# TensorE's order in block 1 written out by hand, with a new head and softmax attention by pairs of heads

## The chip, the core and the metric

One core of a Trainium2 chip runs the whole program. The metric is the device time of one execution in microseconds (us). Five engines work side by side, each through its own instructions in order: TensorE (PE in the profile, its weight loads as PEld), VectorE (DVE), ScalarE (ACT), GpSimd (POOL) and SyncE (SP), which issues most DMAs. This chip can tell differences of about 0.2% of this kernel's time from no change.

## The reference, cut to what matters

Two transformer blocks run on 256 tokens of width 2048, batch 1. Block 1 puts 16 meta tokens in front (272 rows), and everything is float32:

```python
xn = _rms(h, n1)
z_rwkv, z_fox, z_gate = jnp.split(xn @ w_in, (RWKV_COLS, RWKV_COLS + FOX_COLS), axis=-1)
y_a = _rwkv7(z_rwkv + (z_prev - z_rwkv) * mu, ...)   # 16 heads of 64: S = S*w + (S a) b^T + v k^T
y_b = _fox(z_fox, ...)                               # 16 heads of 64: causal softmax with a decay bias
merged = g_a * (y_a @ w_a) + g_b * (y_b @ w_b)       # gates of z_gate
h = h + merged @ w_o
h = h + (silu(gate) * up) @ w_dn                     # gate, up of _rms(h) @ w_gu
```

Block 2 (projections, stick-breaking and chunked softmax attention, an output projection) follows and is not touched.

## The kernel before, in words

Every large product is made of three single-pass matmuls of split operands (`mm3`): `wload` brings 512 KB of weights by a DMA of SP's queue into a `raw` tile (three of them), ACT casts it to `hi`, and DVE subtracts to get `lo` (`split`, lines 219 to 221). `hi` and `lo` have three buffers each. `gemm_a` makes one 128-column tile of a projection, transposed (48 matmuls of 272 columns or fewer, from two chunks of 24); `gemm_b` makes 512 output columns (96 matmuls of 512 columns from eight chunks). Products that are not split are plain float32 matmuls, which the trace shows as two instructions each.

Block 1 works in this order (lines 290 to 813). The head loads the normalised input's raw form and the first weights (`first`: 112, then 96 columns), and builds `xh`/`xl`, the split input. Each of the three later `first` tiles follows only when the one before has its weights. The row norm `rs` is taken out of the matmul and multiplied in afterwards. Then come four groups `q` of four heads: `rwkv(q)` makes six projection tiles, the decays, 4 x 4 x 2 blocks of inner products (`gt`), a triangular inverse of 31 dependent steps on DVE (lines 570 to 582, between two rounds of DMA through DRAM), and then a recurrence over one short and four long stretches (lines 625 to 678). Each stretch is a chain TensorE, DVE, TensorE, ACT and DVE, TensorE, DVE. A group norm (lines 687 to 702), four transposes and a DMA to `ydr` end it. `fox(q)` makes six more tiles and goes through its four heads one after the other: scores, softmax, five transposes, and five small products per head (lines 750 to 787). `gate(n)` are eight `gemm_b` groups. After that, `w_b` and `w_a` multiply the two branches, which come back from `ydr`.

What sets the order: Tile's scheduler. It plays a timeline over all engines and gives each engine, at each moment, the instruction of highest priority that is ready by its estimates; priority is the order of tracing, and weight loads are moved ahead by 300. So TensorE's order, too, comes from the estimates, and small products are strewn between the matmuls of a tile wherever the planner had them ready.

PSUM has four banks for projections (`g`), two for the recurrence (`q`) and two for softmax attention (`f`).

Of the kernel before, what the change touches and what calls it, by code (L numbers as in the profile page):

```python
# [15 lines left out]
D = 2048  # L16
# [7 lines left out]
AHEAD = 300  # L24
BANKS = {"g": 4, "q": 2, "f": 2}
# [82 lines left out]
def prep(i):  # L108
# [51 lines left out]
    l0 = np.concatenate([w[:, 3072:3168], w[:, 6592:6608]], 1)  # L160
    a["w_l0"] = A(l0.reshape(2, 8, 128, 112).transpose(0, 2, 1, 3))
    a["w_l1"] = A(w[:, 3168:3264].reshape(2, 8, 128, 96).transpose(0, 2, 1, 3))
    sel = [w[:, 3264:3520]]
# [33 lines left out]
def body(tc, a, out):  # L197
# [5 lines left out]
    with ExitStack() as top:  # L203
# [21 lines left out]
        def wload(src, n, m, ahead=AHEAD, dst=None, parts=1):  # L225
# [7 lines left out]
            with tc.high_priority(offset=ahead):  # L233
                for i in range(parts):
                    ns, fs = slice(i * n // parts, (i + 1) * n // parts), slice(i * f // parts, (i + 1) * f // parts)
                    latest[0] = nc.sync.dma_start(r3(raw)[:, ns], src[:, ns])  # L236
                    split(raw[:, fs], hi[:, fs], lo[:, fs])
            return r3(hi), r3(lo)

        def mm(o, l, r, start=True, stop=True, **k):  # L240
            P.matmul(o, l, r, start=start, stop=stop, **k)  # L241

# [5 lines left out]
        def gemm_a(chunks, kpc, x, m, n, ready=False):  # L248
            ps = bank("g")
            nk = len(chunks) * kpc  # L250
            for ci, src in enumerate(chunks):
                w = src if ready else wload(src, kpc, m)
# [37 lines left out]
        with ExitStack() as ph:  # L290
            x3 = ph.enter_context(tc.tile_pool(name="x3", bufs=1))
            rp = ph.enter_context(tc.tile_pool(name="rp", bufs=1))
            NTMP, RT0 = 7, META - 2
# [4 lines left out]
            def tmpf(shape):  # L298
                return T(rp, shape, "c", bufs=5)
# [4 lines left out]
            def tmpp(shape):  # L304
                return T(rp, shape, "p", bufs=4)

# [3 lines left out]
            first, xs_ = [], []  # L310
            for j, src in enumerate((a["w_l0"][0], a["w_l0"][1], a["w_l1"][0], a["w_l1"][1])):
                xr = x4()[:, :4 * L].rearrange("p (k t) -> p k t", t=L)
                step = 2 if j == 0 else 4
                for i0 in range(0, 4, step):
                    nc.sync.dma_start(xr[:, i0:i0 + step], a["xT"][:, 4 * j + i0:4 * j + i0 + step])
                    if i0 == 0:
                        first.append(wload(src, 8, 112 if j < 2 else 96, ahead=0, parts=4 // step))
                    for i in range(i0, i0 + step):
# [3 lines left out]
                S.activation(xr, xr, AF.Square)  # L322
                G.tensor_tensor(out=xr[:, 0:2], in0=xr[:, 0:2], in1=xr[:, 2:4], op=ALU.add)
                G.tensor_tensor(out=xr[:, 0], in0=xr[:, 0], in1=xr[:, 1], op=ALU.add)
                xs_.append(xr)
            G.dma_start(ident, a["eye"])
            G.dma_start(ones, a["one"])
            G.dma_start(cst, a["cst"])
            ps = bank()
            for j in range(4):  # L330
                mm(ps[:, :L], ones, xs_[j][:, 0], j == 0, j == 3)
            rs = T(rp, [128, L], "rs")
            S.activation(rs, ps[:, :L], AF.Sqrt, bias=e6, scale=1.0 / D)
            V.reciprocal(rs, rs)
            ps = bank()
            rsn = T(cp, [128, 4], "rsn")
            for t in range(2):
                P.transpose(ps[:, 128 * t:128 * t + 128], rs[:, META + 128 * t:META + 128 * t + 128], ident)
            V.tensor_copy(rsn[:, 0:2], ps[:, 0:256].rearrange("p (t c) -> p t c", c=128)[:, :, 0])
            V.tensor_scalar(out=rsn[:, 2:4], in0=rsn[:, 0:2], scalar1=0.5, scalar2=None, op0=ALU.mult)  # L340
# [10 lines left out]
            xk = lambda kt: (xh[:, kt], xl[:, kt])  # L351
# [22 lines left out]

            lz = T(rp, [128, L], "lz", bufs=2)
            ps = gemm_a(first[:2], 8, xk, 112, L, True)
            shift(ps, 112, 0, lz[:112])
# [18 lines left out]
            ps = bank()  # L396
            for t in range(2):
                P.transpose(ps[:, 16 * t:16 * t + 16], fz[fr, 1, META + 128 * t:META + 128 * t + 128], ident[fr, fr])
            V.tensor_copy(cq, ps[:, :32].rearrange("p (a b) -> p a b", b=16))

            lz = T(rp, [128, L], "lz", bufs=2)
            ps = gemm_a(first[2:], 8, xk, 96, L, True)
            shift(ps, 96, 1, lz[:96])
# [3 lines left out]
            for j in range(2):  # L407
                lz = T(rp, [128, L], "lz", bufs=2)
                shift(next_a(RT0), 128, 2 + j, lz[:, META:], RT0)
# [6 lines left out]
            def to_units(src, dst, tag):  # L416

                ps = bank(tag)
                for j in range(2):
                    for t in range(2):  # L420
                        P.transpose(ps[:, 256 * j + 128 * t:256 * j + 128 * t + 128], src[:, t, 128 * j:128 * j + 128], ident)
                ys = T(rp, [128, 512], "ys" + tag)
                S.copy(ys, ps)
                G.dma_start(dst, ys)

# [5 lines left out]
            def rwkv(q):  # L431
# [7 lines left out]
                for j in range(2):  # L439
                    shift(next_a(), 128, 8 + 6 * q + j, vz[:, j, 48:])  # L440
# [765 lines left out]
```

## Time and profile before

| what | us |
|---|---|
| median of three timed runs | 2049.92 (2048.58 to 2051.02) |
| the profiled execution | 2047.9 |
| its span, first to last instruction | 2046.1 |
| PE busy in the span | 2003.9 (98%) |
| DVE busy | 1223.2 (60%) |
| ACT busy | 954.9 (47%) |
| POOL busy | 156.8 (8%) |

Busy time of PE counts matmuls to their modelled end, so a PE that is busy may still run small products that fill it badly, or run at a lower clock. How well a stretch is used is read from the distance between starts of matmuls. In this trace block 1, with `w_b`, takes the first 731 us; `w_a` starts at 753.

### The profile page before, as it was taken

What the parts mean: (1) busy time and instruction counts of PE and PEld (TensorE: products, weight loads), DVE (VectorE), ACT (ScalarE), POOL (GpSimd) and SP (SyncE); (2) the same over time, 40 slices, a digit from 0 to 9 for tenths busy, and PEclk for the clock granted to TensorE, in tenths of its full rate; (3) what the DMA queues carried; (4) which work ended last, traced back from release to release, by engine and by line L of the source; (5) the groups of instructions that cost most, each with busy time, mean ns of one, the idle gap of its engine ahead of it and who ended that gap; (6) DMA issues with size and microseconds to landing.
All of it is one profiled execution on the core that took longest, in us unless ns stands there. A gap on an engine that the chain in (4) does not pass through costs nothing.

```text
span 2046.1 us, 29715 instructions
## 1 busy us (share of the span) xinstructions
PE 2003.9 (98%) x11478; PEld 1719.1 (84%) x11478; DVE 1223.2 (60%) x2161; ACT 954.9 (47%) x1285; POOL 156.8 (8%) x230
## 2 busy tenths in 40 slices
PE   8999999999999959999999999999999999999998
PEld 7999889889878748888888888888888888998886
DVE  6686777678557547555555544555555565665555
ACT  6545454545444324454444433444444555444443
POOL 3122221231110100000000000000000000000000
PEclk9999999999989979999999999999999999999999
DMA  5544455355446647555555555555555565444554
GB/s 190 184 153 140 147 173 159 126 159 159 139 143 212 227 160 250 188 187 188 192 189 186 193 191 193 194 192 189 186 193 186 180 204 187 146 142 155 183 193 145
DMA packets 118847, 363.28 MB, mean 178 GB/s; under 512 B 28800, under 2 KB 29088, under 8 KB 118704
## 3 DMA queue, kind: packets, MB, share of 16 engines
q1 hardware_dynamic: 113712, 344.98, 51.3%
q0 software_dynamic: 4992, 16.40, 2.6%
q8 instruction: 90, 1.47, 0.3%
q14 instruction: 53, 0.43, 0.1%
HBM read 351.72 MB, written 9.60 MB: 177 GB/s over the span
## 4 chain that ended last, share of the span: by engine, by line
PE 95%; DMA 1%; ACT 1%; issue 1%; DVE 1%; SPq 0%; DVEq 0%; POOL 0%; ACTq 0%; POOLq 0%
PE g L241 85%; PE f L241 4%; PE q L241 4%; DMA raw<-in_w_a 1%; PE q L833 1%; PE f L833 1%; DMA x<-in_xT 0%; ACT hi L220 0%; DVE lo L221 0%; DMA raw<-in_w_b 0%; PE q L559 0%; DVE X L321 0%; SPq L236 0%; PE f L1086 0%; PE q L1086 0%
## 5 line engine op out<-in xcount | busy, mean ns | idle before, releaser
L221 DVE TENSOR_TENSOR lo<-raw,hi 128x1024 fp32r<-128x1024 f32 (+2 forms) x633 | 771.6, 1220 | 611.4 <-ACT hi L220 608.6
L241 PE MATMUL g<-hi,X 128*128 128x512 f32 (+1 forms) x3344 | 1048.5, 392 | 12.6 <-ACT hi L220 12.4
L220 ACT CAST hi<-raw 128x1024 fp32r<-128x1024 f32 (+2 forms) x633 | 661.4, 1045 | 851.7 <-PE g L241 724.7
L241 PEld LDWEIGHTS g<-hi,X 128*128 128x128 f32 x3344 | 626.7, 189 | 143.5 <-issue 16.0
L241 PE MATMUL g<-lo,X 128*128 128x512 f32 (+1 forms) x1672 | 656.3, 393 | 0.9 <-DVE lo L221 0.9
L241 PE MATMUL g<-X,hi 128*128 128x272 f32 (+4 forms) x2176 | 429.7, 293 | 9.1 <-ACT hi L220 5.9
L241 PEld LDWEIGHTS g<-lo,X 128*128 128x128 f32 x1672 | 315.3, 189 | 66.0 <-DVE lo L221 2.5
L241 PEld LDWEIGHTS g<-X,hi 128*128 128x128 f32 (+2 forms) x2176 | 346.7, 191 | 15.8 <-ACT hi L220 5.9
L241 PE MATMUL g<-X,lo 128*128 128x272 f32 (+3 forms) x1088 | 320.6, 295 | 0.0
L241 PEld LDWEIGHTS g<-X,lo 128*128 128x128 f32 (+1 forms) x1088 | 207.6, 191 | 2.7 <-issue 0.7
L241 PE MATMUL g<-hi,Y 128*128 128x512 f32 x544 | 170.9, 390 | 0.0
L241 PEld LDWEIGHTS g<-hi,Y 128*128 128x128 f32 x544 | 102.2, 188 | 20.7
L241 PE MATMUL g<-lo,Y 128*128 128x512 f32 x272 | 106.6, 392 | 0.0
L945 POOL DMA_DIRECT2D cst<-in_cst x1 | 0.5, 543 | 832.8 <-PE g L241 832.8
L241 PEld LDWEIGHTS g<-lo,Y 128*128 128x128 f32 x272 | 51.1, 188 | 10.3
L761 POOL TENSOR_SCALAR p<-ckb,cq,qs 128x144 f32<-128x144 f32 (+1 forms) x32 | 42.9, 1347 | 46.4 <-issue 31.1
L582 DVE TENSOR_TENSOR c<-c 108x42 f32<-108x42 f32 (+31 forms) x236 | 40.5, 206 | 0.3
L579 DVE TENSOR_TENSOR c<-hq,c 108x42 f32<-108x42 f32 (+31 forms) x236 | 39.5, 202 | 1.1 <-DMA hq<-hd 0.9
L367 POOL TENSOR_TENSOR d<-z 128x272 f32<-128x272 f32 (+3 forms) x28 | 23.3, 834 | 136.7 <-DVE z L366 101.7
L768 ACT ACTIVATE p<-p,fst,qs 128x144 f32<-128x144 f32 (+1 forms) x32 | 17.7, 555 | 23.4 <-DVE fst L767 23.0
L241 PEld LDWEIGHTS q<-x,x 64*128 64x128 f32 (+1 forms) x160 | 17.7, 189 | 4.9 <-issue 2.9
L645 POOL TENSOR_TENSOR sp<-sbd,pp 64x128 f32<-64x128 f32 x24 | 14.7, 612 | 88.2 <-DVE sbd L671 57.7
(448 smaller groups left out, 1411.9 us busy)
## 6 DMA issues: line engine op xcount, KB each, us to landing
raw<-in_w_gu SPq DMA_DIRECT2D x176, 512.0 KB
raw<-in_w_A SPq DMA_DIRECT2D x100, 512.0 KB
raw<-in_w_dn SPq DMA_DIRECT2D x88, 512.0 KB
raw<-in_w_g SPq DMA_DIRECT2D x64, 512.0 KB
raw<-in_w_o SPq DMA_DIRECT2D x32, 512.0 KB
raw<-in_w_qk SPq DMA_DIRECT2D x32, 512.0 KB
raw<-in_w_out SPq DMA_DIRECT2D x32, 512.0 KB
raw<-in_w_b SPq DMA_DIRECT2D x16, 512.0 KB
```

Source lines behind the costliest of these rows:

```text
L220: S.copy(hi, src)
L221: V.tensor_tensor(out=lo, in0=src, in1=hi.bitcast(F32), op=ALU.subtract)
L241: P.matmul(o, l, r, start=start, stop=stop, **k)
L367: G.tensor_tensor(out=d[:m, t1:], in0=z[:m, t1:L], in1=z[:m, 1 + t1:], op=ALU.subtract)
L579: V.tensor_tensor(out=t_, in0=hs[:108, j, j + 1:].unsqueeze(1).to_broadcast([108, k_, w]), in1=xs[:, :, j:j + 1].to_broadcast([108, k_, w] ...
L582: V.tensor_tensor(out=xs[:, :, j + 1:], in0=xs[:, :, j + 1:], in1=t_, op=ALU.add)
L645: G.tensor_tensor(out=sp[64 * e:64 * e + 64], in0=blk_(old, e), in1=dec(e), op=ALU.mult)
L761: G.tensor_scalar(out=m_, in0=ckb[:, h, :n], scalar1=cq[:, t, hg:hg + 1], scalar2=qs[:, 0, t, h:h + 1], op0=ALU.subtract, op1=ALU.mult)
L768: S.activation(sm[:, rng[t]], sm[:, rng[t]], AF.Exp, bias=st[:, 1, sidx:sidx + 1], scale=qs[:, 1, t, h:h + 1], accum_out=st[:, 2, sidx:sid ...
L833: P.transpose(ps[:, o:o + 128], src[:, t, 128 * (k + j):128 * (k + j) + 128], ident)
L945: G.dma_start(cst2, a["cst2"])
```

## The change

- **TensorE's order.** Within block 1, `tc.manual_schedule` keeps TensorE's instructions in the order of tracing. The other engines are scheduled as before. The parts of `rwkv` and `fox` that follow the projections become generators. `now` adds up an estimated TensorE time; a generator yields the time after which its next products may be placed, and after every `mm3` of a `gemm` the program resumes those that are due.
- **Order of the large work.** For each q: six tiles of `rwkv`, spawn its task, six tiles of `fox`, spawn its task, then the gates: none, 4, 5, and 6, 7, 0, 1, 2, 3. `turn` keeps two recurrences from overlapping. What is left over after the last gate is placed there.
- **Head.** The first three tiles are made together (weights `w_f`, 336 columns, in eight loads), row by row as input and weights arrive, with three matmuls of zeros ahead of them. The norm becomes a task, and the constants go by SP's queue.
- **Softmax attention** works on pairs of heads: scores of both heads alternate, the probabilities are normalised on DVE before they are transposed, the meta tokens of both heads share one product (`vpad`, `vd`), and the output comes out transposed, so `to_units` is not needed for it.
- **Buffers.** `xx`, `gnw` and `ysf` have their own tiles; tag `c` has four buffers, not five.

```diff
+GATES = ((), (4,), (5,), (6, 7, 0, 1, 2, 3))
+        now, tasks = [0.0], []
+        def pump():
+            while True:
+                due = [k_ for k_ in tasks if k_[0] <= now[0]]
+                if not due:
+                    return
+                k_ = min(due, key=lambda k_: k_[0])
+                try:
+                    k_[0] = now[0] + next(k_[1])
+                except StopIteration:
+                    tasks.remove(k_)
+        def spawn(task):
+            tasks.append([now[0], task])
+            pump()
         def mm(o, l, r, start=True, stop=True, **k):
             P.matmul(o, l, r, start=start, stop=stop, **k)
+            now[0] += (12 + int(np.prod(r.shape[1:])) * (1 if r.dtype == F32R else 4) / 2.4) / 1e3
                     mm3(ps[:m, :n], [t[:, j] for t in w], x(kt), kt == 0, kt == nk - 1)
+                    pump()
+            ph.enter_context(tc.manual_schedule(engines={mybir.EngineType.PE}))
+            wz = tmpf([128, 512])
+            V.memset(wz, 0.0)
+            ps = bank()
+            for _ in range(3):
+                mm(ps, wz[:, :128], wz)
+            FIRST = ((0, 112, 0), (112, 96, 0), (208, 128, RT0))
+            pf = [bank("g") for _ in FIRST]
...
+                        for p_, (c0, m, t0) in zip(pf, FIRST):
+                            mm3(p_[:m, :L - t0], [t_[:, i - i0, c0:c0 + m] for t_ in w], (xh[:, kt, t0:], xl[:, kt, t0:]), kt == 0, kt == 15)
...
+            def rwkv(q, kz, rz, vz):
                 wl = wload(a["w_lora"][q], 4, 256)
+                yield 2.0
...
+                yield 9.0
...
+                yield 14.0
+                while turn[0] != q:
+                    yield 1.0
...
+                yield 46.0
...
+                        yield 1.8
...
+                        yield 1.6
...
+                    yield 2.4
+                turn[0] = q + 1
...
+                yield 16.0
                 to_units(yf, ydr[0][q], "q")
...
+                    yield 3.0
+                    sc = [bank("f") for _ in range(2)]
                     for t in range(2):
+                        for e in range(2):
+                            er = slice(64 * e, 64 * e + 64)
+                            mm(sc[e][:, rng[t]], qn[er, j, 128 * t:128 * t + 128], kn[er, j, :144 + 128 * t])
...
+                    yield 11.0
...
+                    yield 2.2
+                    yb = bank("f")
+                    mm(yb[:, :256], vd[:, 128 * j:128 * j + 128], pm, True, False, skip_group_check=True)
+                    for e in range(2):
+                        mm(yb[64 * e:64 * e + 64, :256], vn[:, 0, 128 * j + 64 * e:128 * j + 64 * e + 64], pts[e][:, 0:256], False, False, skip_group_check=True)
+                    for e in range(2):
+                        mm(yb[64 * e:64 * e + 64, 128:256], vn[:, 1, 128 * j + 64 * e:128 * j + 64 * e + 64], pts[e][:, 256:384], False, True, skip_group_check=True)
...
+            for q, gates in enumerate(GATES):
+                spawn(rwkv(q, *rwkv_in(q)))
+                spawn(fox(q, *fox_in()))
                 for n in gates:
                     gate(n)
+            while tasks:
+                now[0] += 0.5
+                pump()
```

## Rows read from the trace of the kernel before

**Rows 1.** The page: busy us, share of the span, instructions, by engine.

```profile
PE 2003.9 (98%) x11478; PEld 1719.1 (84%) x11478; DVE 1223.2 (60%) x2161; ACT 954.9 (47%) x1285; POOL 156.8 (8%) x230
```

**Rows 2.** TensorE's waits: for what, us in total, times, longest.

```profile
PE q L241 <- DVE g__2826 L651: 1.4, 1, 1.4
```

**Rows 3.** Windows: stretch, us, then busy us of PE, PEld, DVE, ACT, POOL, granted clock, DMA.

```profile
0.00:20.00 20.00, 10.87 (x35) 8.14 (x36) 11.41 (x25) 13.01 (x24) 8.08 (x17) 1.00 0.72 248
...
100.00:150.00 50.00, 50.00 (x396) 47.48 (x394) 43.20 (x151) 22.86 (x36) 12.86 (x12) 1.00 0.50 155
...
350.00:400.00 50.00, 48.63 (x370) 44.55 (x369) 33.35 (x61) 26.55 (x41) 7.50 (x11) 0.93 0.39 134
...
550.00:600.00 50.00, 50.00 (x258) 37.84 (x256) 23.67 (x55) 18.17 (x35) 8.51 (x13) 0.90 0.38 120
...
700.00:750.00 50.00, 31.85 (x181) 24.90 (x179) 24.52 (x41) 13.29 (x20) 2.99 (x6) 0.83 0.43 145
```

**Rows 4.** Timeline of TensorE, head: start, us, what, count, idle before and its releaser.

```profile
5.87 0.80 PE L241 MATMUL g<-X,hi 128*112 128x272 f32 x2 [5.87 <-ACT hi L220]
...
21.62 0.88 PE L241 MATMUL g<-X,hi 128*96 128x272 f32 x3
22.30 0.43 PE L241 MATMUL g<-X,lo 128*96 128x272 f32 x1
...
24.30 0.41 PE L241 MATMUL g<-X,hi 128*96 128x272 f32 x2
24.55 0.29 PE L241 MATMUL g<-X,lo 128*96 128x272 f32 x1
...
42.41 0.42 PE L241 MATMUL g<-X,hi 128*128 128x272 f32 x2
```

**Rows 5.** Timeline of ACT in the head.

```profile
17.61 0.82 ACT L220 CAST hi<-raw 128x768 fp32r<-128x768 f32 x1
18.34 1.76 ACT L320 ACTIVATE X<-x,vec 128x272 fp32r<-128x272 f32 x4
20.00 1.09 ACT L322 ACTIVATE x<-x 128x1088 f32<-128x1088 f32 x1
```

**Rows 6.** One window of the head; the last number is the DMA rate in GB/s.

```profile
12.00:14.00 2.00, 1.16 (x3) 0.63 (x3) 1.74 (x2) 1.88 (x4) 1.92 (x2) 1.00 1.03 412
```

**Rows 7.** Timeline of TensorE: one head's small products, then the next head's scores.

```profile
147.33 0.43 PE L241 MATMUL f<-vm,p 16*128 16x64 f32 x2
...
149.00 0.97 PE L241 MATMUL f<-f 64*128 64x144 f32 x4
149.90 0.51 PE L241 MATMUL g<-X,hi 128*128 128x258 f32 x2
```

**Rows 8.** Timeline of TensorE: products whose neighbours use other halves of the array.

```profile
107.55 1.16 PE L241 MATMUL q<-x,x 64*128 64x128 f32 x16
108.64 0.40 PE L241 MATMUL g<-X,hi 128*128 128x272 f32 x1
...
718.50 0.45 PE L241 MATMUL q<-uv,kb 128*64 128x64 f32 x8
718.78 0.40 PE L241 MATMUL q<-uv,gt 128*64 128x64 f32 x6
```

**Rows 9.** Timeline of TensorE, end of block 1.

```profile
730.35 0.81 PE L241 MATMUL q<-uv,gt 128*64 128x64 f32 x8 [0.36 <-ACT uv L656]
...
753.26 1.19 PE L241 MATMUL g<-hi,X 128*128 128x512 f32 x2 [12.44 <-ACT hi L220]
```

**Rows 10.** Timeline of ACT where the gates give way to `w_b`.

```profile
684.12 1.05 ACT L220 CAST hi<-raw 128x1024 fp32r<-128x1024 f32 x1 [4.04 <-DMA raw<-in_w_b]
```

**Rows 11.** The page's costliest groups: count, busy us, mean ns, idle before.

```profile
L221 DVE TENSOR_TENSOR lo<-raw,hi 128x1024 fp32r<-128x1024 f32 (+2 forms) x633 | 771.6, 1220 | 611.4 <-ACT hi L220 608.6
L582 DVE TENSOR_TENSOR c<-c 108x42 f32<-108x42 f32 (+31 forms) x236 | 40.5, 206 | 0.3
L579 DVE TENSOR_TENSOR c<-hq,c 108x42 f32<-108x42 f32 (+31 forms) x236 | 39.5, 202 | 1.1 <-DMA hq<-hd 0.9
```

More of the change, by code (lines that the diff above doesn't have):

```diff
@@ L223, in body, with wload @@
         more_raw, latest = [], [None]
-        def wload(src, n, m, ahead=AHEAD, dst=None, parts=1):
+        def wload(src, n, m, ahead=AHEAD, dst=None, parts=1, between=None):
             f = n * m
@@ L309, in body, with squares @@
             x4 = lambda: T(rp, [128, 4 * LP], "x4", bufs=4)
-            first, xs_ = [], []
-            for j, src in enumerate((a["w_l0"][0], a["w_l0"][1], a["w_l1"][0], a["w_l1"][1])):
-                xr = x4()[:, :4 * L].rearrange("p (k t) -> p k t", t=L)
[L313 to L318, printed above, removed]
+            wz = tmpf([128, 512])
[5 more added lines that the diff above has]
+            pf = [bank("g") for _ in FIRST]
+            xs_ = []
+            def squares(xr):
+                S.activation(xr, xr, AF.Square)
+                G.tensor_tensor(out=xr[:, 0:2], in0=xr[:, 0:2], in1=xr[:, 2:4], op=ALU.add)
+                G.tensor_tensor(out=xr[:, 0], in0=xr[:, 0], in1=xr[:, 1], op=ALU.add)
+            for j in range(4):
+                xr = x4()[:, :4 * L].rearrange("p (k t) -> p k t", t=L)
+                xs_.append(xr)
+                for i0 in range(0, 4, 2):
+                    step = 1 if j + i0 == 0 else 2
+                    if j == 0 or i0 == 0:
+                        n = 1 if j + i0 == 0 else 2 if j == 0 else 4
+                        nc.sync.dma_start(xr[:, i0:i0 + n], a["xT"][:, 4 * j + i0:4 * j + i0 + n])
+                    w = wload(a["w_f"][2 * j + i0 // 2], 2, 336, ahead=0, parts=2 if j + i0 == 0 else 1, between=(lambda: nc.sync.dma_start(xr[:, 1:2], a["xT"][:, 1:2])) if j + i0 == 0 else None)
+                    for i in range(i0, i0 + 2):
                         kt = 4 * j + i
@@ L328, in body @@
[L328 to L331, printed above, removed]
+                        for p_, (c0, m, t0) in zip(pf, FIRST):
+                            mm3(p_[:m, :L - t0], [t_[:, i - i0, c0:c0 + m] for t_ in w], (xh[:, kt, t0:], xl[:, kt, t0:]), kt == 0, kt == 15)
+                if j == 0:
+                    nc.sync.dma_start(ones, a["one"])
+                    nc.sync.dma_start(ident, a["eye"])
+                    nc.sync.dma_start(cst, a["cst"])
+                else:
+                    squares(xs_[j - 1])
@@ L340, in body, with norm @@
-            V.tensor_scalar(out=rsn[:, 2:4], in0=rsn[:, 0:2], scalar1=0.5, scalar2=None, op0=ALU.mult)
+            def norm():
+                yield 1.5
+                ps = bank()
+                for j in range(3):
+                    mm(ps[:, :L], ones, xs_[j][:, 0], j == 0, False)
+                for i in range(4):
+                    mm(ps[:, :L], ones, xs_[3][:, i], False, i == 3)
+                S.activation(rs, ps[:, :L], AF.Sqrt, bias=e6, scale=1.0 / D)
+                V.reciprocal(rs, rs)
+                yield 12.0
+                ps = bank()
+                for t in range(2):
+                    tr(ps[:, 128 * t:128 * t + 128], rs[:, META + 128 * t:META + 128 * t + 128], ident)
+                V.tensor_copy(rsn[:, 0:2], ps[:, 0:256].rearrange("p (t c) -> p t c", c=128)[:, :, 0])
+                V.tensor_scalar(out=rsn[:, 2:4], in0=rsn[:, 0:2], scalar1=0.5, scalar2=None, op0=ALU.mult)
@@ L342, in body @@
+            spawn(norm())
             rks = T(rp, [128, 8, 2], "rks")
@@ L395, in body, with gate_by_token @@
             cq = T(rp, [128, 2, 16], "cq")
[L396 to L399, printed above, removed]
+            def gate_by_token():
+                yield 12.0
+                ps = bank()
+                for t in range(2):
+                    tr(ps[:, 16 * t:16 * t + 16], fz[fr, 1, META + 128 * t:META + 128 * t + 128], ident[fr, fr])
+                V.tensor_copy(cq, ps[:, :32].rearrange("p (a b) -> p a b", b=16))
+            spawn(gate_by_token())
             lz = T(rp, [128, L], "lz", bufs=2)
-            ps = gemm_a(first[2:], 8, xk, 96, L, True)
-            shift(ps, 96, 1, lz[:96])
+            shift(pf[1][:96, :L], 96, 1, lz[:96])
             ta = T(rp, [96, 2, L], "ta", F32R)
@@ L799, in gate @@
                 G.dma_start(gdr[n], g_)
-            prev = None
-            for q, gates in enumerate(((), (4, 5), (6,), (7, 0, 1, 2, 3))):
-                cur = rwkv(q)
-                next(cur)
-                if prev is not None:
-                    next(prev)
-                next(cur)
-                prev = cur
-                fox(q)
-                if q == 3:
-                    next(prev)
+            for q, gates in enumerate(GATES):
+                spawn(rwkv(q, *rwkv_in(q)))
+                spawn(fox(q, *fox_in()))
                 for n in gates:
                     gate(n)
+            while tasks:
+                now[0] += 0.5
+                pump()
         yp = pool("yp")
```

230 lines of the change are left out of this document (120 added, 110 removed).

## The prediction, made before the result was known

> **What bounds the kernel now.** I read the page's busy shares first: TensorE is busy for 98% of the span and no other engine above 60% [rows 1]. So a gain must come from TensorE's idle time, from its clock, or from small products that take more of it than their columns need. The windows say where: the first 20 us have TensorE busy for 10.9, and 700 to 750 for 31.9; in the middle of block 1 it is all but full, but the granted clock is 0.93 and 0.90 in two windows of 50 us [rows 3]. Then the timelines of TensorE at both ends [rows 4, 9], and of the small products [rows 7, 8]. TensorE's list of waits is short: inside a recurrence the longest was 1.4 us, once [rows 2]. The block after it is untouched and I cost it at nothing.
>
> **The head (term A).** Before, the first product starts at 5.87, and the matmuls come 0.226 us apart ((22.30 - 21.62)/3) until after 22, then 0.125 ((24.55 - 24.30)/2); 272 columns at 2.4 GHz are 0.113 and at 1.2 GHz 0.227, so the head runs at the lower level, although the clock column reads 1.00 there [rows 3, 4]. Up to then TensorE had pauses: 9.1 of 20 us idle. Four tiles are done at 42.41. After: 144 matmuls of the three tiles at 0.125 are 18.0 us. ACT's share is 16 x 0.44 for the input (1.76/4), 8 x 0.72 for 672 columns of weights (0.82 x 672/768) and 4 x 1.09 of squares, 17.2 us [rows 5]. The DMAs bring 2.2 MB of input, 2.8 of weights and 0.43 of constants, which now stand in SP's queue ahead of part of them (1.0 us): 5.4 MB at 412 GB/s are 13.1 us [rows 6]. So TensorE bounds, ACT close behind. The zeros, three products of 512 columns, are six instructions of two passes: 0.226 x 512/272 x 2 is 0.85 us at the lower level, 5.1 in all, from about 1.2 (an estimate: DVE's memset stands first) to 6.3. They end as the first data is there, and their price, some 0.5 us, is in the start. 6.3 + 18.0 + 1 for gaps is 25. The fourth tile (48 x 0.12 = 5.8) and the norm, now seven products of 0.45 (3.2), make it 34 in place of 42.4: **-8**. If the clock rises only where it did, 144 x 0.226 are 32.5 and the term is +5; without a gap -10.
>
> **The end (term B).** Before, the last recurrence ends TensorE's work at 731.2 (730.35 + 0.81); group norm, transposes, a trip through DRAM and the first `w_a` weights follow one another, and the next dense matmul is at 753.26, after an idle time of 12.44 [rows 9]: 22 us. After: in the written order the last task has 132.5 us of delays (2.0 + 3.2 + 9 + 14 + 4 + 4 + 3.6 + 1.5 + 46 + 2 + 4 + 23.2 + 16), and 33 resumptions that each wait for the end of an `mm3` (some 8 us); its own products are about 15. Behind its spawn stand six tiles (288 x 0.125 = 36 us) and six gates (576 x 0.235 = 135, at 0.125 x 512/272 per matmul), 171 us before any small work. So it ends well before the last gate, its group norm and DMA are covered by gates, and the 22 us go. What is late next is the step from the gates to `w_b`: its input is split into the place of `xl`, so not before the last gate, and meanwhile `ydr` holds two of three `raw` tiles. ACT waited 4.04 us for `w_b` there [rows 10], which small products of the last recurrence partly covered; that cover is gone: +4 (0 to +8). **-18**.
>
> **Softmax attention (term C).** Before, one head's five products take 1.67 us (147.33 to 149.00) and the next head's scores 0.90 (to 149.90) [rows 7]: 5.14 a pair. After, scores of a pair are 2 x 416 columns of four passes, 1.39 us at 2.4 GHz; the output has one product of 256 columns over both heads (0.43) and, per head, 256 and 128 columns (1.28 for both). Neighbours that use other rows or columns of the array overlap in the trace: 16 instructions of 128 columns (0.107 each, 1.71) took 1.09, and eight of 64 (0.43) took 0.28, both about 0.65 [rows 8]. So 0.9 + 0.43 + 0.84; two more interruptions and a dearer transposition of the meta columns (estimates) are 0.55. 2.7 in place of 5.1, for eight pairs: **-19**. With no overlap 3.65 a pair, -12; with full overlap 2.3, -23. On DVE the normalising is new, 416 columns a head, 0.5 us by the 1220 ns of 1024 columns [rows 11], 8 us in all; it lies beside gates and tiles unless a product waits for it (term E). The Trainium skill (TensorE: Matmul & The Clock Gate, Part 3, The mechanism) has matmuls on different row groups run together with 4 ns between starts. By it the scores would be 0.7, and the term 2 us larger; the 1.09 above lies between that and no overlap.
>
> **The clock in the middle (term D).** 0.93 and 0.90 over 50 us cost 3.5 and 5.0 us [rows 3]; one dip follows the 1.4 us wait [rows 2], others follow the slow products of softmax attention, which get denser. I take **-6** of the 8.5 (0 to -8.5).
>
> **Waits in the written order (term E).** Before, a product that was not ready was passed over by the planner; now it holds all behind it on TensorE, tile matmuls too, and through full `hi`/`lo` buffers ACT's casts and SP's loads. There are 44 resumptions per group, 176 in all. 156 are short steps with 1.0 to 3.0 us allowed, against a DVE operation or two and at worst a split of 1.22 in front [rows 11]. Twenty are tight: 14.0 ahead of `gt`, 46.0 over the inverse and 16.0 over the group norm, four times each, and 11.0 over the softmax, eight times. In the 46 us DVE has the 31 steps (80.0/4 = 20 us), splits at 1.22 for 24 x 0.125 = 3.0 us of matmuls (41%), so 27 us free for 20 of steps and the softmax beside them: little room [rows 11]. The nearest price is the wait of 1.4 us with its dip of 3.5, about 5 [rows 2, 3]. Below: 0. Above: all twenty late, 100. I take 0.5 for each of the twenty and 3 for the rest, **+13**, nearer to the low end, since the planner's order had one such wait.
>
> **Sum.** -8 - 18 - 19 - 6 + 13 = -38. The profiled execution took 2047.9, so 2010; the runs' median is 2.0 above it, so **2012**.
>
> **Rivals.**
> 1. *Waits outweigh the gains.* DVE, filled by splits, the 31 steps and the softmax, is late at the tight places, TensorE stands and its clock falls. Price 5 us each; 51 us of gains are gone from the tenth on, beside the rest. All of the twenty: 2012 - 13 + 100 = 2099; at twelve to fifteen 2059 to 2074, slower. For it: the 27 us above, and DVE busy for 43.2 of the 50 us in which the first group's steps run [rows 3]. Against: the planner placed the same work with one wait of 1.4. The skill's rule, same page and part, that matmuls start and end strictly in program order, is what makes a wait hold the tiles; here it would give those 2059 to 2074. Before's trace, where the planner chose the order, can't test it. 15%: 11 slower, 2 the same, 2 still faster.
> 2. *Hardly any waits*, overlap as good as rows 8 or better: 2012 - 13 - 4 - 4 = 1991. For it: TensorE's few waits. 25%.
> 3. *The head stays at the lower clock*, because data comes in pieces: 2012 + 13 = 2025. For it: the pauses of before [rows 4]. Against: the zeros. 10%.
> 4. *The end does not close*: the change doesn't do what it says, since the last recurrence or the `w_b` loads still come late: 2012 + 18 = 2030. Against: 171 us of cover. 8%.
>
> **How the numbers follow.** The forecast has 42%, with its own range 2002 to 2023. A difference of 0.2%, 4 us, is what can be told from none. Faster: 42 + 25 + 10 + 8 + 2 = 87%; same 2%; slower 11%. The range 1987 to 2038 leaves out the slower rival and the far end of the second.
>
> **What would show it.** A: first split products near 6 us with 0.125 between starts by 8, and the fifth tile begun near 34. B: no idle time above 5 us between the last gate and `w_a`. C: a pair's scores in about 0.9 us, its output in about 1.3. D: no slice of block 1 below 0.95. E: TensorE's list of waits names DVE and ACT tiles of `rwkv` and `fox` with 10 to 20 us in total; above 50, rival 1 holds. Wrong altogether: a kernel whose dense stretches, past block 1, have moved.

## The result, and the profile after

The kernel after took 2035.45 us (median of 4, 2034.67 to 2037.02), the kernel before 2049.25 beside it: ratio 0.9935, interval 0.9917 to 0.9952. So it gained 14 us where 38 were forecast: the time is outside the forecast's own range of 2002 to 2023, and inside the wide one, which ends at 2038. Below, times are of the profiled executions (span 2033.8 after, 2046.1 before).

The windows of [rows 3], after (same columns):

```profile
0.00:20.00 20.00, 14.44 (x63) 10.49 (x64) 10.68 (x26) 12.99 (x25) 8.00 (x17) 0.91 0.84 279
100.00:150.00 50.00, 49.06 (x419) 46.83 (x418) 40.10 (x131) 22.14 (x33) 18.24 (x22) 0.97 0.42 133
350.00:400.00 50.00, 48.71 (x384) 45.54 (x383) 35.69 (x115) 27.55 (x40) 5.93 (x7) 0.97 0.50 155
550.00:600.00 50.00, 46.55 (x327) 33.99 (x327) 32.09 (x100) 25.10 (x47) 9.42 (x17) 1.00 0.51 156
700.00:750.00 50.00, 46.59 (x201) 37.43 (x202) 27.91 (x28) 20.92 (x20) 2.12 (x4) 1.00 0.77 251
```

The end of the block, the last window, is filled: 46.59 us of work at a clock of 1.00 against 31.85 at 0.83. The middle has lost: between 550 and 600 us TensorE is busy for 46.55 of 50 us, where before had all 50, though at a clock of 0.90. The whole middle, after and then before:

```profile
41.00:650.00 609.00, 577.48 (x4491) 511.39 (x4492) 440.76 (x1261) 306.96 (x492) 129.36 (x171) 0.97 0.48 151
41.00:650.00 609.00, 607.16 (x4442) 539.42 (x4441) 433.22 (x1199) 308.90 (x477) 124.26 (x163) 0.98 0.49 156
```

TensorE's list of waits between 41 and 650 us (for what, us in total, times, longest) says on what; before has two rows for the same stretch, of 1.4 ([rows 2]) and 0.4:

```profile
PE f L263 <- DVE p L873: 10.2, 4, 4.0
PE q L263 <- DVE gt L589: 5.2, 7, 1.6
PE f L267 <- DVE p L873: 4.0, 3, 3.2
PE q L263 <- DVE uv L739: 2.7, 5, 0.8
PE f L267 <- DVE pm L882: 2.5, 4, 0.9
PE q L263 <- DVE uvm L718: 2.3, 3, 1.5
```

Here `p` are the normalised probabilities of softmax attention and `pm` their meta columns, transposed; `gt`, `uv` and `uvm` belong to the recurrence. A wait is often followed by a stretch at the lower clock. These are the first pair's transpositions on TensorE's timeline, and the windows around them:

```profile
156.41 0.37 PE L267 MATMUL f<-ident,p 128*32 128x128 f32 x1 [3.17 <-DVE p L873]
158.59 0.61 PE L263 MATMUL f<-ident,p 128*32 128x128 f32 x2 [1.81 <-DVE p L873]
```

```profile
155.90:162.60 6.70, 4.38 (x18) 3.15 (x19) 6.06 (x35) 1.94 (x5) 0.00 (x0) 0.50 0.48 163
164.00:200.00 36.00, 33.91 (x354) 29.85 (x350) 26.12 (x73) 19.51 (x38) 5.99 (x9) 1.00 0.39 113
```

The clock column is 0.50 for 6.7 us, the lower of TensorE's two levels (1.2 and 2.4 GHz), and 1.00 after it. Between 43 and 650 us after has eight such stretches, 3.4 or 6.8 us each, every one begun within a wait of 0.6 us or more or less than 2 us behind it. Other waits have none behind them, such as one of 1.94 at 558.84. Before has four stretches, one of them behind its wait of 1.4.

The end itself, on TensorE's timeline, answers to [rows 9]:

```profile
693.02 0.50 PE L263 MATMUL g<-hi,X 128*128 128x512 f32 x1 [1.71 <-ACT X L220]
697.33 0.50 PE L263 MATMUL g<-lo,X 128*128 128x512 f32 x1 [0.48 <-DVE lo L221]
701.31 0.73 PE L263 MATMUL g<-hi,X 128*128 128x512 f32 x2 [1.43 <-ACT hi L220]
702.57 0.50 PE L263 MATMUL g<-lo,X 128*128 128x512 f32 x1 [0.53 <-DVE lo L221]
...
741.77 0.70 PE L263 MATMUL g<-hi,X 128*128 128x512 f32 x2 [1.05 <-issue]
```

The first `w_a` product is at 741.77 in place of 753.26. From there to the end of TensorE's last product after takes 1283.7 us and before 1284.6, so block 1 has all but 1 us of the difference. The table splits the time from 43 us to that product, worked out from TensorE's instructions: *idle* is time in which no matmul runs, before and after 650 us (a wait across 650 counts where it begins); *lost* is half of the busy time within stretches whose granted clock is 0.5; *work* is the rest, what the products themselves take at the full clock.

```
kernel                              w_a at  idle<650  idle>650  lost   work   median us
before                              753.3      1.8      22.6    10.7   675.1   2049.25
after                               741.8     31.5       5.3    17.0   645.0   2035.45
softmax attention alone (x8_fox)    749.4      6.8      29.5     8.9   661.1   2044.42
after, planner (x1_planner)         742.5      2.8      29.2     4.5   663.0   2035.87
gt, bonus later (x2_gt)             735.8     27.7       3.8    19.3   642.0   2025.02
first pair later (x3_pair)          740.3     29.2       4.1    18.8   645.1   2031.88
both, and state later (x4_both)     720.1     22.9       3.2     6.8   644.1   2015.06
the same, more edits (x10_all)      724.8     25.6       4.0     5.9   646.3   2020.29
x4_both, POOL's order (x16_pool4)   719.9     19.9       4.2     7.7   645.2   2016.90
x4_both, delays x 1.25 (x14_loose4) 735.9     32.8       4.8    12.3   643.2   2030.32
POOL's order (x5_pool)              736.9     25.4       3.8    19.5   645.2   2029.76
delays x 1.5 (x13_loose)            748.9     23.1      25.5    13.8   643.6   2041.97
small product between (x12_between) 743.3     26.3       4.4    14.6   655.0   2036.40
planner, then written (x15_hybrid)  755.9     37.3       4.9    18.6   652.2   2047.11
```

After against before: idle at the end -17.3, work -30.1, idle in the middle +29.7, lost at the lower clock +6.3; -11.4 together. The 1.5 us that the head gained are in the work, since at 43 us after is that much further. The columns are of one execution each. The intervals of the ratios below are some 3.5 us either way, so that two versions less than some 5 us apart are not told from equal by their times alone.

### The profile page after: what moved, and what is told of

Read it like the earlier page. It is cut to its first block, busy times and chain, and to the rows that moved or that the text cites. A ratio compares the mean times of both kernels' runs of the same rounds, so it can differ in the third digit from the quotient of the medians.

```text
span 2033.8 us, 29647 instructions
## 1 busy us (share of the span) xinstructions
PE 1981.4 (97%) x11410; PEld 1698.3 (84%) x11410; DVE 1223.3 (60%) x2188; ACT 954.3 (47%) x1290; POOL 152.6 (8%) x226
## 4 chain that ended last, share of the span: by engine, by line
PE 86%; DVE 6%; DMA 4%; ACT 2%; issue 1%; POOL 1%; SPq 0%; DVEq 0%; ACTq 0%
PE g L263 78%; PE f L263 3%; DVE lo L221 3%; PE q L263 3%; DMA raw<-in_w_b 1%; PE f L267 1%; ACT hi L220 1%; PE q L267 1%; DVE xx L658 1%; DMA raw<-in_w_a 1%; POOL p L854 1%; DVE c L655 1%; DMA raw<-in_w_g 0%; DMA x<-in_xT 0%; DVE gt L589 0%
## 5 line engine op out<-in xcount | busy, mean ns | idle before, releaser
L221 DVE TENSOR_TENSOR lo<-raw,hi 128x1024 fp32r<-128x1024 f32 (+1 forms) x635 | 772.9, 1218 | 604.4 <-ACT hi L220 599.9
L220 ACT CAST hi<-raw 128x1024 fp32r<-128x1024 f32 (+1 forms) x635 | 661.4, 1042 | 817.5 <-PE g L263 679.9
L263 PE MATMUL g<-X,hi 128*128 128x272 f32 (+3 forms) x2176 | 430.3, 296 | 3.3 <-ACT hi L220 3.1
L263 PEld LDWEIGHTS g<-X,hi 128*128 128x128 f32 (+1 forms) x2176 | 347.1, 193 | 10.7 <-ACT hi L220 3.6
L655 DVE TENSOR_TENSOR c<-hq,xx 108x42 f32<-108x42 f32 (+31 forms) x236 | 40.3, 204 | 9.7 <-DMA hq<-hd 9.4
L658 DVE TENSOR_TENSOR xx<-xx,c 108x42 f32<-108x42 f32 (+31 forms) x236 | 40.8, 203 | 0.4
L267 PE MATMUL f<-ident,p 128*128 128x128 f32 (+1 forms) x64 | 14.5, 333 | 6.6 <-DVE p L873 4.0
L1028 ACT ACTIVATE th<-g,r2h 128x512 f32<-128x512 f32 x22 | 15.1, 685 | 9.9 <-PE g L263 9.9
```

The source lines that it names most:

```text
L220: S.copy(hi, src)
L221: V.tensor_tensor(out=lo, in0=src, in1=hi.bitcast(F32), op=ALU.subtract)
L267: P.transpose(o, i, eye)
L655: V.tensor_tensor(out=t_, in0=hs[:108, j, j + 1:].unsqueeze(1).to_broadcast([108, k_, w]), in1=xs[:, :, j:j + 1].to_broadcast([108, k_, w] ...
L658: V.tensor_tensor(out=xs[:, :, j + 1:], in0=xs[:, :, j + 1:], in1=t_, op=ALU.add)
L1028: S.activation(th[:, t], pgt[t], AF.Tanh, scale=r2h[:, t:t + 1])
```

## The experiments

**The softmax attention alone (x8_fox).** Kernel before, head and planner as they were, with the new `fox`.

> The kernel before with the new softmax attention alone: head and planner as before. The prediction's term C (-19 as work, -6 to -10 with the clock's dips in the middle): about 2021. Theory O (the planner doesn't put a pair's scores next to each other, so their overlap, 0.8 us a pair, is lost, and only the meta and output products are cheaper, about -9, with up to -10 from dips of the clock that followed the old small products): 2030 to 2040. The hole of 21 us ahead of the first w_a product stays in both.

Measured: 2044.42, ratio 0.9979 [0.9968, 0.9990], a smaller gain than either theory gave. The windows (columns as above):

```profile
41.00:650.00 609.00, 606.36 (x4447) 530.38 (x4446) 429.47 (x1134) 311.75 (x484) 124.59 (x163) 1.00 0.52 163
650.00:750.00 100.00, 66.27 (x422) 52.30 (x422) 56.93 (x167) 31.06 (x44) 7.83 (x16) 0.77 0.47 159
```

In the middle it did what terms C and D say: work is 14.0 us less, and the clock reads 1.00 for all of 41 to 650 us, so the 10.2 us lost there before are gone. But 20 of these 24 us come back. A wait of 5.05 for the input of `w_b` that begins at 649 is new, the end has 6.9 more idle time in smaller waits, and loses 8.4 more at the lower clock. What a step gains ahead of the hole at the end mostly makes the hole wider: the last recurrence ends at 726.9, only 4.3 us earlier than before, and from 707 on TensorE waits for its tiles (`sbd`, `uv`, `uvm`). That its chain of small steps sets the end is read from these waits; no run here shortens the chain.

**The written order taken out (x1_planner).**

```diff
-            ph.enter_context(tc.manual_schedule(engines={mybir.EngineType.PE}))
```

> The changed kernel with TensorE's order left to the planner again (tracing order, head, softmax by pairs and buffers as in the change). Theory W (TensorE stands at a few places of the written order, and its clock falls behind each wait; together some 36 us): the planner passes over what is not ready, TensorE's waits in block 1 fall from 27 to under 8 us and the half-clock stretches from 37 us to about 20, so 2035 less 20 to 25, about 2012, unless the end opens again. Rival R (DVE and POOL are behind by as much whatever the order, the waits only show where): the time stays within 4 us of 2035. A third outcome: the hole at the end of block 1 comes back and costs 15 to 20 us, 2045 to 2055.

Measured: 2035.87, 0.9934 [0.9916, 0.9951], the same as after, by another way: the time is rival R's, the middle is as theory W has it, and the hole of the third outcome is back. First the middle, then TensorE's timeline at the end:

```profile
41.00:650.00 609.00, 608.07 (x4481) 532.75 (x4480) 438.27 (x1211) 315.94 (x490) 124.89 (x163) 1.00 0.51 162
```

```profile
727.04 1.09 PE L267 MATMUL q<-ident,c 128*128 128x128 f32 x4 [8.58 <-DVE c L787]
742.46 1.19 PE L263 MATMUL g<-hi,X 128*128 128x512 f32 x2 [14.34 <-ACT hi L220]
```

The planner has no idle time in the middle (608.07 of 609; after has 577.48) and no stretch at the lower clock, but the hole at the end, 8.58 and 14.34, as in before. So with the new code the written order as such is worth nothing: it gives 23.9 us of idle time at the end, and with it 18.0 of work, which I had not expected, and pays 28.7 of idle time in the middle and 12.5 at the lower clock.

**Longer delays (x2_gt, x3_pair, x4_both).** The tasks yield longer ahead of products that waited: x2_gt at `gt`'s products and the bonus, x3_pair ahead of a first pair's transpositions, x4_both both, with 3.0 for 1.6 behind the recurrence's start.

```diff
-                    yield 2.0                                  # gt (x2_gt, x4_both)
+                    yield 4.0
...
-                yield 1.5                                      # bonus (x2_gt, x4_both)
+                yield 3.0
...
-                    yield 11.0                                 # softmax (x3_pair, x4_both)
+                    yield 16.5 if j == 0 else 11.0
```

> One kind of place given more time: the delays around the inner products of the recurrence (2.0 becomes 4.0 twice, 1.5 becomes 3.0). W: the waits on gt (5.2 us in seven) and the four half-clock stretches behind them (20.4 us long, 10.2 us lost) go, 2035 - 15 = 2020, between 2016 and 2026. R: the waits turn up at the next product instead, 2032 to 2037.

> The delay over the softmax of the first pair of each group is 16.5 in place of 11.0; the second pair keeps 11.0. W: the waits for the normalised probabilities (14.2 us) and for the meta copy behind them (2.5) go, with three half-clock stretches (13.7 us long, 6.8 lost): 2035 - 21 = 2014, between 2010 and 2024. R: 2032 to 2037, since the second pair or the recurrence is then late.

> Both lengthenings and 3.0 in place of 1.6 ahead of the first state of the recurrence (waits of 2.3 us). W: the gains add, 2035 - 15 - 21 - 3 = 1996, between 1994 and 2010, with less than 8 us of waits of TensorE in block 1 and at most two half-clock stretches. R: 2030 or more.

Measured: 2025.02 (0.9882 [0.9864, 0.9899]), 2031.88 (0.9913 [0.9894, 0.9932]) and 2015.06 (0.9833 [0.9817, 0.9849]). Each edit removed the waits that it aimed at, and others appeared: x3_pair has no wait for `p` left, but 6.1 us for `pm`. x2_gt's time lies in theory W's range, but not for theory W's reason: its lost time did not fall (19.3 against 17.0). x4_both lies between the two theories. The two edits alone give 10.4 and 3.6, together with the third 20.4; the 6.4 us above their sum are no more than the noise of these medians, and the third edit has a part in them. In the profiled executions idle time falls by 8.6 from after to x4_both, and lost time from 17.0 to 6.8. In x4_both the list of waits begins with

```profile
PE f L267 <- DVE pm L882: 8.9, 7, 2.6
PE q L263 <- DVE g__2593 L732: 2.0, 1, 2.0
```

and most of these waits stand alone, with no lower clock behind them. This version is faster than both kernels, clear of noise, and has 34 of the 38 us that were forecast.

**More room still (x14_loose4, x13_loose, x10_all).** In x14_loose4 the delays of x4_both are multiplied by 1.25, in x13_loose those of after by 1.5. In x10_all, x4_both has all of a pair's transpositions ahead of the copies out of their banks, and the head's DMAs of x7_order.

```diff
-                k_[0] = now[0] + next(k_[1])
+                k_[0] = now[0] + 1.5 * next(k_[1])
```

> The kernel after with every delay of the written order multiplied by 1.5. The four groups then take 1.5 times 132.5 us of delays each, so the last recurrence ends later, at 650 to 680 in place of 611, still ahead of the last gate. Theory W (waits in the middle, 31.5 us of idle time and 17 us lost at half clock, come from delays that are too short): idle time in the middle below 12, half clock below 5 us lost, 2035 - 19 - 12 = 2004. Rival D (DVE, ACT and POOL are full, so that a wait only moves to the next product, as with the version of all fixes, whose idle time in the middle was 25.6): 2015 to 2030. Rival E (the order is now so late that the end opens again): w_a after 745, 2040.

> The version with the longer delays at gt, the bonus, the state and the first pairs (2015), with every delay multiplied by 1.25. Theory W: its idle time in the middle (22.9 us) halves, 2003. Rival D: the waits move, 2010 to 2018.

> The version with the longer delays at gt, the bonus, the state and the first pairs (the two changes run before, together), and with two more: the head's DMAs as in the run beside it, and in a pair's transpositions all eight are issued ahead of the copies out of their banks, with 3.0 in place of 2.2 behind them. Theory W (every wait in the written order costs itself and often a dip of the clock, and goes where the order leaves room): the 8.9 us of waits for pm go, the head gives 4, so 2015 - 9 - 4 = 2002. Rival (DVE is full and a wait only moves to the next product): 2011 to 2017, with as many us of waits as before.

Measured: 2041.97 (0.9975 [0.9963, 0.9988]), 2030.32 (0.9925 [0.9903, 0.9947]), 2020.29 (0.9862 [0.9843, 0.9882]). Theory W misses in all three; in x14_loose4 and x10_all the rival's time was too low as well. x13_loose shows rival E: the last recurrence ends behind the gates and the hole is back, 8.57 and 13.11. x14_loose4 has 32.8 us of idle time, more than x4_both, and its longest wait is for work that had not waited at all:

```profile
PE q L263 <- ACT kbm L641: 9.9, 3, 5.1
PE f L267 <- DVE pm L882: 7.6, 6, 3.0
```

A delay is not slack: it moves a product, and all that hangs on it on DVE and ACT, beside other work. In x10_all the waits for `pm` went and others came (5.8 for the group norm's `c`, 2.4 for `p`); idle time in the middle rose by 2.7. Of the 5 us by which x10_all is slower than x4_both, 1.5 are its head's: the fifth tile begins at 42.24 in place of 40.77.

**POOL's order (x5_pool, x16_pool4).** After issues the bias of both pairs with all eight multiplications first, as POOL's timeline shows; the first pair's scores have ended by 143.30. Here the second pair's bias stands behind the first pair's.

```profile
134.20 10.33 POOL L854 TENSOR_SCALAR p<-ckb,cq,qs 128x144 f32<-128x144 f32 x8 [9.88 <-ACT lz L820]
145.35 3.18 POOL L855 TENSOR_TENSOR p<-p,cst 128x128 f32<-128x128 f32 x7
```

```diff
+                    with (tc.issue_after(last_bias.ins) if j else ExitStack()):
...
-                                G.tensor_tensor(out=m_[:, n - 128:], in0=m_[:, n - 128:], in1=fm, op=ALU.add)
+                                last_bias = G.tensor_tensor(out=m_[:, n - 128:], in0=m_[:, n - 128:], in1=fm, op=ALU.add)
```

> The kernel after with one order added on POOL: the second pair's bias is issued behind the whole of the first pair's (in the kernel after the eight multiplications of both pairs stand first, so the first pair's bias ends 4 to 5 us after its scores). Theory P (the 16 us of waits at the first pairs come from that order): the first pair's bias ends 5 us earlier, the waits of pairs 0, 2, 4 and 6 (4.98, 4.99, 3.53, 2.71) fall below 1 each, with two of their dips; about -15, 2020. Rival V (DVE's other work in front of the softmax holds it): waits as they were, 2034.

> The version with the longer delays (2015) and POOL's order as in the run on it (5.7 us on the kernel after). Theory W: its first pairs wait little already (16.5 us of delay), so 0 to -4, 2013. Rival D: the second pair's bias is now the late one, 2018.

Measured: 2029.76 (0.9917 [0.9902, 0.9932]) and 2016.90 (0.9850 [0.9833, 0.9866]). On after the waits for `p` fall from 14.2 us to 2.2, so theory P has the cause of the largest row in the list; but it gave 6 us by the medians (4 by the ratios to before), not 15: `pm` now takes 5.6, and lost time stays (19.5). On x4_both it changes nothing that can be measured.

**Do a pair's scores run together (x11_apart, x12_between).** After, a pair's scores take 0.91 us, where before a single head's took 0.90 ([rows 7]). x11_apart swaps the loops, so that both products of one head stand first; x12_between also puts a small product over all rows between the heads.

```diff
-                    for t in range(2):
-                        for e in range(2):
+                    for e in range(2):
+                        for t in range(2):
...
+                        if e == 0:
+                            mm(sc[e][:, 416:418], ident, ident[:, 0:2])
```

> The kernel after, with the loops around a pair's scores swapped: both query tiles of one head first, then those of the other, so that neighbours in TensorE's order use the same rows of the array. Nothing else is changed. Theory O (the written order gains because partners on different rows stand next to each other and run together; after, a pair's eight score products start in twos 10 ns apart and take 0.8 us, where the planner's order, which puts another product between the two heads, has 1.66): 0.8 us more for each of eight pairs, about +7, so 2042. Theory W (only the waits matter, and the scores stand beside them): no change, 2035, and the waits for the softmax 0.8 us shorter each.

> The kernel after with the heads of a pair's scores one after the other, as in the run before, and between them one small product over all 128 rows (two columns, into unused columns of the bank). Theory O2 (partners on different rows run together even if two products of the same rows stand between them, as the run before showed with 0.98 us in place of 0.97, but not across a product that uses all rows, which is what the planner put there): a pair's scores take 1.66 us and the small product 0.1, so +0.8 for each of eight pairs, +6 in all, 2041. Rival (the overlap doesn't depend on what stands between): 1.1 us a pair, +1, 2036.

Measured: 2035.80 (0.9930 [0.9912, 0.9948]) and 2036.40 (0.9958 [0.9940, 0.9977]). TensorE's timeline of a pair's scores, in after:

```profile
142.39 0.97 PE L263 MATMUL f<-f 64*128 64x144 f32 x8
143.30 0.39 PE L263 MATMUL g<-X,hi 128*128 128x258 f32 x1
```

and in x12_between:

```profile
142.20 0.97 PE L263 MATMUL f<-f 64*128 64x144 f32 x4
143.10 0.38 PE L263 MATMUL f<-ident 128*128 128x2 f32 x2
143.41 0.97 PE L263 MATMUL f<-f 64*128 64x144 f32 x4
144.31 0.51 PE L263 MATMUL g<-X,hi 128*128 128x258 f32 x2
```

x11_apart tells nothing by its time, since the overlap stayed (0.92 us a pair). x12_between shows theory O2 in its rows: the small product parts the heads, a pair takes 2.11 us, and work rises by 10.0. Yet the median rose by 1 only, and the first `w_a` product by 1.5: idle time in the middle fell by 5.2, lost time by 2.4. (By the ratios to the kernel before, 0.9958 against 0.9935, the rise is nearer 5, with an interval as wide.) So in this execution work that TensorE saves in the middle of this order is mostly given to waits: what the products wait for is made by DVE, ACT and POOL.

**Planner first, written order last (x15_hybrid, x17_hybrid4).**

```diff
             for q, gates in enumerate(GATES):
+                if q == 3:
+                    ph.enter_context(tc.manual_schedule(engines={mybir.EngineType.PE}))
```

> The kernel after with the planner for the first three groups and the written order from the fourth on. Theory M (the written order pays in the middle, with 31.5 us idle and 17 at half clock against the planner's 2.8 and 0, and earns at the end, with 5.3 us idle against 29.2 and 4.5 at half clock): the planner's 742.5 at the first w_a product, less 24 and 4.5 at the end, plus some 5 for the fourth group's own waits: w_a at 719, about 2012. Rival J (both orders need their whole run: at the change of order tasks of the third group stand on the wrong side, and the end opens again): 2030 to 2040.

> Planner for the first three groups, the written order with the longer delays and POOL's order in the fourth. Theory M: as the first of these three runs, less 5 for the fourth group's waits, 2007. Rival J: 2030 to 2040.

Measured: 2047.11 (0.9985 [0.9974, 0.9995]) and 2041.18 (0.9967 [0.9954, 0.9980]); theory M misses, rival J has the place. Windows and timeline of x15_hybrid:

```profile
41.00:400.00 359.00, 357.82 (x2878) 324.98 (x2877) 270.57 (x747) 193.26 (x313) 89.85 (x117) 1.00 0.50 157
400.00:460.00 60.00, 30.89 (x251) 25.57 (x250) 30.70 (x154) 10.76 (x21) 4.47 (x10) 0.59 0.22 59
```

```profile
411.35 1.08 PE L267 MATMUL q<-ident,c 128*128 128x128 f32 x4 [6.14 <-DVE c L786]
...
448.72 0.28 PE L263 MATMUL q<-c,gt 32*32 32x32 f32 x2 [19.31 <-DVE c L675]
```

Up to 400 us the planner's part is full. Then the hole stands at the change of order, and the end is closed (4.9). In both places where the planner's part ends, here and at the end of x1_planner, it has used up the projections that it may move and leaves the recurrence's chain of small steps for last.

**The head (x7_order, x6_nozeros, x18_squares).** x7_order: input in pieces of 272 KB, constants last. x6_nozeros: without the three products of zeros. x18_squares: squares written behind the casts.

> The kernel after with the head's DMAs in another order: each piece of the input is two rows of tiles (272 KB) in place of four, and the constants (416 KB) stand behind all of the head's loads. Theory S (the head is late because the fifth input tile's 544 KB piece stands behind the constants, and only 156 to 243 GB/s move in the first 9 us; its wait of 3.1 us and the 3.4 us at half clock behind it go): the fifth tile begins at 37 in place of 40.9, about 2031. Theory A (ACT bounds the head, full from 15 to 24 us): the wait at 15 is shorter, but the tile begins at 40 or later, 2035.

> The kernel after without the head's three products of zeros. Theory Z (they put TensorE's clock up before the first data is there, so that from 6.5 us on products stand 0.125 apart where before they stood 0.226 apart until 22): without them 0.226 apart until some time behind the wait at 15, and the fifth tile begins at 43 to 46 in place of 40.9. Rival (the head is bound by data that comes late, and a slower TensorE only waits less): 41, within 1.

> The kernel after with the squares of the norm behind all casts of the head on ACT (3.3 us of squares stand between 15 and 22 us of the kernel after, ahead of the casts of the last weights). Theory A (ACT's order bounds the head from 15 us on, where it is busy without a gap until 24): the last weights are cast 2 to 3 us earlier and the fifth tile begins at 38 to 39. Theory R (the three buffers of the raw weights and the DMA bound it: SP waited 12.8 us for them): 40 to 41.

Measured, fifth tile begun at: after 40.89, x7_order 43.02, x6_nozeros 41.53, x18_squares 41.32 (medians 2039.34 with 0.9949 [0.9932, 0.9965], and one run each of 2032.85 and 2034.39, which says nothing at this size). The rows of x7_order on TensorE:

```profile
20.75 0.50 PE L263 MATMUL g<-X,hi 128*112 128x272 f32 x2 [2.63 <-ACT hi L220]
22.54 0.57 PE L263 MATMUL g<-X,lo 128*112 128x272 f32 x1 [1.28 <-DVE lo L221]
```

The wait at 15 is gone and stands at 20, where the casts of later input and the squares are ahead of the weights' on ACT. Without the zeros the products are 0.226 apart, the lower level, until 12, and the tile is only 0.6 us later, as the rival has it. x18_squares is no test: ACT's order is still the planner's, which put the squares back.

## Why the prediction was wrong

**The failed step is term E, with D's sign behind it.** Waits in the written order were +13 and the middle's clock -6, +7 together. They measured 29.7 us of added idle time and 6.3 of added loss, +36. The difference of 29 is more than the miss of 24. Rival 1 had the mechanism, though the gains outweighed it. Wrong was the size, in two ways. Of the twenty tight places, priced at 0.5 each, only four waited, the softmax of each group's first pair, but 14.2 us in all. What made them late was an engine that the term does not name: POOL, 8% busy, with the bias of both pairs in one go (x5_pool: 2.2 us left of the 14.2). The planner's trace passes over a product that isn't ready, and so has no row for how late its inputs are. And I took the 156 short steps for safe, at 3 in all: `gt` (behind 2.0 and 1.5), `uv`, `pm`, `uvm` and the like took some 15. D by itself had the right sign (x8_fox: 1.00 throughout, 10.2 us back, more than the 6) and was then lost again to E's waits: on average 0.54 us more at the lower clock for each us of idle time in the middle (17.0 by 31.5), less than the 3.5 for 1.4 that I took from before. That the waits are what cost the time x4_both shows: with shorter waits, and work as in after, it takes 2015.06.

**A, -8, came to -1.5.** The zeros work: 0.125 us between starts from 6.5 on. But the head isn't bound by TensorE: without the zeros, with products at the lower level until 12, it is only 0.6 us later (x6_nozeros). After, the tiles' 144 products end at 31.73, not 25:

```profile
15.45 0.51 PE L263 MATMUL g<-X,hi 128*112 128x272 f32 x2 [3.10 <-ACT hi L220]
...
40.89 0.49 PE L263 MATMUL g<-X,hi 128*128 128x272 f32 x2
```

The input that this waits for came late to ACT, and the last weights later still:

```profile
12.99 1.76 ACT L364 ACTIVATE X<-x,vec 128x272 fp32r<-128x272 f32 x4 [2.81 <-DMA x<-in_xT]
...
27.61 0.76 ACT L220 CAST hi<-raw 128x672 fp32r<-128x672 f32 x1 [3.29 <-DMA raw<-in_w_f]
```

The DMA rate of 412 GB/s that I used ([rows 6]) is not that of the head's first loads, small pieces and constants: with the DMA engines as busy (the number before the last), the first windows moved less (the last):

```profile
6.00:9.00 3.00, 2.96 (x19) 2.24 (x17) 1.39 (x3) 1.91 (x4) 0.00 (x0) 1.00 0.98 243
9.00:12.00 3.00, 2.48 (x18) 2.15 (x18) 0.89 (x2) 1.19 (x2) 1.60 (x2) 1.00 1.01 390
```

A sum of bytes over a rate has no order in it. x7_order changed that order and moved the wait; that the three buffers for raw weights, which let input overtake weights, hold the rest is argued from SP's waits for `lo`, which frees them (8.7 us by 25), and was not tried. The 12.8 us in the expectation of x18_squares is the time over which SP issued four loads of weights, not all of it waiting.

**B, -18, was right:** idle time behind 650 us fell by 17.3, the hole of [rows 9] went and the predicted new waits (+4) measure 4.2.

**C, -19.** The new softmax attention alone took 14.0 us of work off under the planner, near the low end of its range. There two of the eight pairs' scores overlap wholly and two in part: the eight take 11.9 us together, after 7.2, and the 4.7 between them are most of what is missing. In the written order the recurrence's small products overlap more, too. By kind, counted from each start to the next, the change is softmax -15, recurrence -9, and the projections' 960 matmuls of 512 columns, interrupted less often, -4 (239 ns apart in place of 243); counted from end to end softmax has -20 and recurrence -8, so the shares are rough. The term's mechanism was right and its place too narrow. That A and C together, -27, came near the -30.1 of work is luck: what A lacked was made good by products that C did not count. As x12_between suggests, most of such work is not time as long as the waits stand.

**The sum** was also wrong in kind. It added what each edit does alone; but x8_fox gave back 20 of 24 us, and x12_between hid 8 of 10 in its profiled execution. Before the hole at the end is closed, and where waits set the pace, terms don't add here. Rival 2 (1991) needs x1_planner's middle with after's end and work: 43 + 645.0 + 2.8 + 5.3 is 696 for `w_a`; no run reached it.

## What to carry to other kernels

When a planner's order is replaced by a written one, the trace of before can't price the waits: it shows only what the planner let through, so measure the lateness of each input first (when its producer ends against when its consumer could start), on every engine, the lightly loaded ones too, and set each delay from that. (Not tried here: x4_both took its delays from the list of waits of after.) Look for where an order runs out of filler: a planner that uses it early leaves the longest chain bare at its end, and gains ahead of that chain buy little (x8_fox kept 4 of 24 us). Tune delays one place at a time, with the list of waits beside each, since a factor on all of them made it slower in both versions where it was tried.

## What the runs showed of the hardware

- Products on different halves of the rows run together almost wholly: 0.91 us for twice 0.90. They do so even out of order: in x11_apart TensorE's order has products of 144, 272, 144, 272 columns, and both of 144 start 13 ns apart, at 141.613 and 141.626, ahead of either of 272 (141.962). The Trainium skill (TensorE: Matmul & The Clock Gate, Part 3, The mechanism) has matmuls start strictly in program order; across row groups this trace doesn't agree. A product over all rows parts them: in x12_between a pair then takes 2.11 us.
- Around two waits for `gt` of 1.1 and 1.6 us, which ended at 224.8 and 228.2, the clock went to the lower level, for 6.8 us; in x4_both waits of 2.6 (at 159 us) and 2.3 (at 415) were followed by no such stretch. What decides it is open.
- DMA engines that were 0.98 busy moved 243 GB/s in one stretch of the head, and engines that were 1.01 busy 390 in the next.
